# A hybrid decoder layer: TensorE in the order of the source, or in the scheduler's

## The chip, the cores and the metric

The kernel runs on one core of a Trainium2 chip. The metric is the device time of one execution in microseconds; three runs of the kernel before the change took 2751.72, 2754.8 and 2756.76 us, a median of 2754.8. One further execution was recorded by the hardware profiler, and all views below are of that one. The engines are called PE (TensorE, matrix products), PEld (its weight loads), DVE (VectorE), ACT (ScalarE), POOL (GpSimd) and SP (SyncE, which here issues the DMA transfers).

## The reference

One decoder layer over 2048 tokens of 1024 features, batch 1, all in float32:

```python
mod = silu(c) @ w_ada + b_ada                       # six vectors of 1024
sh1, sc1, ga1, sh2, sc2, ga2 = split(mod, 6)
h  = rms_norm(x, g_attn) * (1 + sc1) + sh1
z  = h @ w_in                                       # q, k, v of both head groups, gates
ya = swa_attention(...)          # 8 heads of 64, window 128, ALiBi, sinks, 2 kv heads
yb = forgetting_attention(...)   # 8 heads of 64, causal over all keys, F = cumsum(log_sigmoid(f))
x  = x + ga1 * (concat(ya, yb) @ w_out)
h2 = rms_norm(x, g_mlp) * (1 + sc2) + sh2
u  = causal_dwconv(h2 @ w_up, conv_w, conv_b)       # width 3, 5632 channels
a, g = split(u, 2)
x  = x + ga2 * ((silu(g) * a) @ w_down)
y  = rms_norm(x, g_final)
```

## The kernel before

The tokens are cut into four blocks of 512 (n = 0 to 3). Each block has three stages. s1 makes the projections (products at L623 and L651; L276 for the first block), s2 is the attention, s3 is the output projection, the MLP's up-projection with its convolution (products at L1301) and the down-projection (output and down-projection share L1183). Float32 operands are split into a high and a low part in a faster format (wh and wl, hh and hl, ph and pl, ah and al), and each dense product is three matrix products: high by high, high by low, low by high.

The attention of a block is a list of units. A unit of the forgetting attention (a head, or half the queries of a head for n = 2 and 3) makes its scores (s, L968), which ACT and DVE read, biased, into tiles t; DVE keeps their running maximum mx (L951, L959). PE transposes mx (mt, L993), DVE reduces it to m, and PE spreads m over all rows (mb, L1000). ACT copies that (mm, L1007), DVE subtracts it from each t (L1014), ACT takes the exponential (L1019), DVE adds up the sums acc (L1029). Then, group by group of 512 columns, ACT casts t into ph (L728), DVE makes pl (L729), and PE multiplies both by the values into one accumulator o (L1063, L1066). The sums are transposed (lt, L1039), inverted (rl) and spread (mb again); yo (L1072 to L1074) reads o and the unit is stored. There are 48 such units, 8 each for n = 0 and 1 and 16 each for n = 2 and 3. Units of the sliding-window attention (L798 to L868) follow them.

The order of the work is written out by hand. `merge(main, side, ratio)` pulls dense work from one generator, with its cost in microseconds at each `yield`, and slips attention steps from another between, so that the attention keeps to a set share of the dense work. `s2` decides the steps by a clock of its own (`clock`) and by tables of gaps and delays for each block (GAPS, TAS, TBS, LATS, SGAPS). So s2(0) stands among s1(1) and s1(2), s2(1) among s3(0), s2(2) among s1(3) and s3(1), s2(3) among s3(2); s3(3) has nothing beside it. The calls stand in the last lines of the function. "The last merge" below is s3(2) with s2(3).

The framework schedules at build time: on each engine it takes, of the instructions whose operands and buffers its own timing model has ready, the one that comes first in the source. The line `tc.manual_schedule(engines={PE})` holds PE to the order of the source instead. Here it covers the whole kernel. ACT, SP and POOL have no such line over the whole kernel, nor has DVE; two short stretches hold DVE (and in the first one SP) too: `first_groups` and the end of the last block.

PSUM, into which PE writes, is cut into four buffers "d" for dense sums, three "s" shared by scores, mt, mb, lt and the small sums sd, and one "o". The tiles ph and pl have three buffers each (PB), t has ten (NT).

Of the kernel before, what the change touches and what calls it, by code (L numbers as in the profile page):

```python
# [70 lines left out]
def tile_decoder_layer(  # L71
# [42 lines left out]
        return t[:, :w]  # L114

    nc.scalar.preload_act_table_set("exp_and_others")
    ctx.enter_context(tc.manual_schedule(engines={mybir.EngineType.PE}))

    def side_ps(w=512):
        t = pa.tile([P, 512], F32, tag="s", name="sd", bufs=3)  # L120
# [1439 lines left out]
```

## Time and profile before

| what | value |
|---|---|
| median of three runs | 2754.8 us |
| the profiled execution's own time | 2755.67 us |
| its span, first to last instruction | 2754.0 us |
| mean granted clock of TensorE | 0.967 |
| busy: PE, DVE, ACT | 2566.3, 1930.8, 1491.7 us |
| moved by DMA | 588.26 MB |

In the views a line number is that of the kernel before. A row of the timeline has start, length, engine, line, operation, output and inputs, sizes, count, and in brackets the idle time just before with what ended it. A row of waits reads: who waited for whom, total us, times, longest. In a group of instructions the numbers after the count are total busy us and mean ns of one, then the idle time just before them. PE's instructions overlap at their ends, so the price of one in a stream is the distance between two starts, not its length.

### The profile page before, as it was taken

The numbers are of one execution on the slowest core, as the hardware profiler recorded it, in microseconds if no ns is written. First come the engines' busy times: TensorE is split into PE (matmuls) and PEld (weight loads), VectorE is DVE, ScalarE is ACT, GpSimd is POOL, SyncE is SP. The second block draws the span as 40 slices with busy tenths as digits, with TensorE's granted clock in tenths as the row PEclk, the third lists the DMA queues.
The fourth block names the chain that finished last, engine by engine and source line by source line (L and its number), as shares of the span: only waits on it lengthen the run. The fifth ranks groups of instructions, "written<-read, shape, count | busy, mean of one in ns | idle before, by whom it ended". The sixth has DMA issues, their size and how long they took to land.

```text
span 2754.0 us, 38503 instructions
## 1 busy us (share of the span) xinstructions
PE 2566.3 (93%) x12852; PEld 2168.5 (79%) x12852; DVE 1930.8 (70%) x3813; ACT 1491.7 (54%) x3085; POOL 93.1 (3%) x171
## 2 busy tenths in 40 slices
PE   7999888799989999988999999989999999999998
PEld 5878786677877877877788887878888887788887
DVE  6467656789878657776888865879989876344433
ACT  5456564565556666556555665576666666422222
POOL 0001000100000000000000000100000000000000
PEclk9999999899999999999999999999999999999999
DMA  7967579756646786675667779735555576655564
GB/s 234 296 181 234 153 216 306 237 178 200 198 150 201 218 263 204 210 245 166 211 225 228 236 255 300 274 119 179 182 186 180 180 243 218 249 196 196 188 228 183
DMA packets 424515, 588.26 MB, mean 214 GB/s; under 512 B 32380, under 2 KB 272756, under 8 KB 424316
## 3 DMA queue, kind: packets, MB, share of 16 engines
q1 hardware_dynamic: 424316, 585.79, 65.8%
q8 instruction: 102, 1.67, 0.3%
q14 instruction: 97, 0.79, 0.1%
HBM read 440.95 MB, written 144.71 MB: 213 GB/s over the span
## 4 chain that ended last, share of the span: by engine, by line
PE 75%; DVE 8%; DMA 7%; ACT 5%; issue 2%; SPq 1%; POOL 1%; DVEq 0%; POOLq 0%; ACTq 0%
PE d L1301 33%; PE d L1183 19%; PE d L623 6%; PE s L968 4%; DMA wada<-in_w_ada_dram 2%; PE o L1063 2%; PE o L1066 2%; PE d L651 2%; DVE wl L379 1%; DMA q<-qd 1%; DMA wr<-in_w_in_dram 1%; PE mb L1000 1%; PE d L276 1%; PE s L798 1%; DVE pl L729 1%
## 5 line engine op out<-in xcount | busy, mean ns | idle before, releaser
L1301 PE MATMUL d<-hh,wkh 128*128 128x512 f32 (+1 forms) x920 | 355.4, 386 | 6.3 <-ACT hh L110 6.3
L1301 PE MATMUL d<-hl,wkh 128*128 128x512 f32 (+1 forms) x920 | 354.7, 386 | 3.7 <-DVE hl L538 2.7
L1301 PE MATMUL d<-hh,wkl 128*128 128x512 f32 (+1 forms) x920 | 352.1, 383 | 0.0
L379 DVE TENSOR_TENSOR wl<-wr,wh 128x1024 fp32r<-128x1024 f32 (+5 forms) x184 | 219.2, 1192 | 113.9 <-ACT wh L378 99.4
L728 ACT CAST ph<-t 128x512 fp32r<-128x512 f32 (+2 forms) x304 | 178.2, 587 | 188.8 <-PE o L1063 185.9
L378 ACT CAST wh<-wr 128x1024 fp32r<-128x1024 f32 (+5 forms) x184 | 188.5, 1025 | 169.0 <-PE d L1301 78.6
L985 ACT ACTIVATE t<-s,bc 128x256 f32<-128x256 f32 (+3 forms) x464 | 204.5, 480 | 103.3 <-DVE t L979 49.7
L1331 ACT ACTIVATE u<-d,cb,cw 128x512 f32<-128x512 f32 x176 | 136.7, 777 | 223.2 <-PE d L1301 217.7
L1334 DVE SCALAR_TENSOR_TENSOR u<-d,cw,u 128x511 f32<-128x511 f32 x176 | 130.8, 743 | 158.9 <-ACT u L1331 158.2
L729 DVE TENSOR_TENSOR pl<-t,ph 128x512 fp32r<-128x512 f32 (+2 forms) x304 | 195.8, 646 | 37.7 <-ACT ph L728 36.5
L1301 PE MATMUL d<-hh,wh 128*128 128x512 f32 (+1 forms) x552 | 215.7, 391 | 2.2 <-ACT hh L110 2.2
L1301 PE MATMUL d<-hl,wh 128*128 128x512 f32 (+1 forms) x552 | 214.2, 388 | 0.4
L968 PE MATMUL s<-q,kkb 128*128 128x256 f32 (+2 forms) x1024 | 198.6, 309 | 16.8 <-DMA q<-qd 16.8
L1301 PE MATMUL d<-hh,wl 128*128 128x512 f32 (+1 forms) x552 | 213.1, 386 | 0.0
L1301 PEld LDWEIGHTS d<-hh,wkh 128*128 128x128 f32 x920 | 174.4, 190 | 39.3 <-ACT hh L110 8.8
L1301 PEld LDWEIGHTS d<-hl,wkh 128*128 128x128 f32 x920 | 174.1, 189 | 38.1 <-DVE hl L538 7.5
L1301 PEld LDWEIGHTS d<-hh,wkl 128*128 128x128 f32 x920 | 174.2, 189 | 33.5
L1063 PE MATMUL o<-ph,vvb 128*128 128x256 f32 (+2 forms) x512 | 153.9, 318 | 27.7 <-DVE yo L1073 27.7
L1019 ACT ACTIVATE t<-t 128x512 f32<-128x512 f32 (+2 forms) x304 | 168.5, 598 | 13.4 <-DVE t L1018 7.2
L968 PEld LDWEIGHTS s<-q,kkb 128*128 128x128 f32 x1024 | 153.7, 197 | 24.5 <-DMA q<-qd 16.4
L623 PE MATMUL d<-hh,wh 128*128 128x512 f32 x360 | 146.2, 406 | 2.6 <-DVE lf L666 2.2
L623 PE MATMUL d<-hl,wh 128*128 128x512 f32 x360 | 143.9, 400 | 2.9 <-DVE hl L538 2.9
(232 smaller groups left out, 6128.5 us busy)
## 6 DMA issues: line engine op xcount, KB each, us to landing
wkh<-wsu SPq DMA_DIRECT2D x110, 512.0 KB
wkl<-wsu SPq DMA_DIRECT2D x110, 512.0 KB
wr<-in_w_up_dram SPq DMA_DIRECT2D x66, 512.0 KB
wkh<-wsd SPq DMA_DIRECT2D x55, 512.0 KB
wkl<-wsd SPq DMA_DIRECT2D x55, 512.0 KB
wr<-in_w_in_dram SPq DMA_DIRECT2D x49, 512.0 KB
wada<-in_w_ada_dram SPq DMA_DIRECT2D x96, 256.0 KB
wsu<-wh SPq DMA_DIRECT2D x44, 512.0 KB
```

What stands on the lines that cost most here:

```text
L378: nc.scalar.copy(wh, raw)
L379: nc.vector.tensor_sub(wl, raw, r32(wh))
L623: nc.tensor.matmul(ps, a[:, k, :], b[k], start=(k == 0 and i == 0), stop=(k == KT - 1 and i == 2),)
L728: nc.scalar.copy(ph[:, e0:], src[:, e0:])
L729: nc.vector.tensor_sub(pl[:, e0:], src[:, e0:], r32(ph[:, e0:]))
L968: nc.tensor.matmul(ps[:, o + low(c0) : o + w], st["kks"][kb // 4][:, (kb % 4) * P : (kb % 4 + 1) * P], qs[a][:, low(c0) : w], start=(a == ...
L985: nc.scalar.activation(tt[:, plain : o + w], ps[:, plain : o + w], AF.Identity, bias=bias(kb))
L1019: nc.scalar.activation(t1, t1, AF.Exp)
L1063: nc.tensor.matmul(po[:, c:], v, ph[:, o + c : o + w], start=(kb == 0), stop=False)
L1183: nc.tensor.matmul(acc[t], l[:, ts], r[:, k % 2, :], start=(i == 0 and l is ah and r is wh), stop=(i == n_k - 1 and l is al),)
L1301: nc.tensor.matmul(ps[:, c], w[a][:, k, :], b[k][:, c], start=(k == 0 and i == 0), stop=(k == KT - 1 and i == 2),)
L1331: nc.scalar.activation(u, ps, AF.Identity, bias=cb[:, ci : ci + 1], scale=c2)
```

## The change

One line goes: PE is no longer held to the source's order, and the framework's scheduler orders it as it does the other engines. Work, tiles, buffers and the source's order, which still gives the priorities, are the same. The two short stretches that hold DVE and SP stay.

```diff
     nc.scalar.preload_act_table_set("exp_and_others")
-    ctx.enter_context(tc.manual_schedule(engines={mybir.EngineType.PE}))
 
     def side_ps(w=512):
```

Of the 12,808 matrix products of the program 7,939 stand at another place in PE's order, 2,980 by more than 20 places and 449 by more than 100; the farthest comes 168 later and 233 earlier. The last 226 stand where they stood. DVE, ACT, POOL and SP have the same instructions in a changed order. In the changed kernel the line numbers are one lower behind the line that went, and the buffer numbers two lower: mb_21286 at L1000 becomes mb_21284 at L999.

The first place is in the last merge, on PE, ahead of a unit's mt. Before (16 rows of this list lie between the last score, s_20512, and mt):

```order
L1301 MATMUL d_20490<-hl_18457,wkh_20239 128x512
L1301 MATMUL d_20490<-hh_18456,wkl_20241 128x512
L1301 MATMUL d_20490<-hh_18468,wkh_20239 128x512
L1301 MATMUL d_20490<-hl_18469,wkh_20239 128x512
L1301 MATMUL d_20490<-hh_18468,wkl_20241 128x512
L1063 MATMUL o_20436<-ph_20462,vvb_19245 128x256
L1066 MATMUL o_20436<-pl_20463,vvb_19245 128x256
L1063 MATMUL o_20436<-ph_20462,vvb_19245 128x256
L1066 MATMUL o_20436<-pl_20463,vvb_19245 128x256
L993 MATMUL mt_20543<-ident_87,mx_20311 128x128 x2
L968 MATMUL s_20549<-q_20300,kkb_19928 128x256 x4
```

Now (60 rows lie between the last score, s_20510, and mt):

```order
L1300 MATMUL d_21030<-hl_18443,wkh_20776 128x512
L1300 MATMUL d_21030<-hh_18442,wkl_20778 128x512
L1300 MATMUL d_21030<-hh_18454,wkh_20776 128x512
L1300 MATMUL d_21030<-hl_18455,wkh_20776 128x512
L1300 MATMUL d_21030<-hh_18454,wkl_20778 128x512
L1300 MATMUL d_21030<-hh_18466,wkh_20776 128x512
L1300 MATMUL d_21030<-hl_18467,wkh_20776 128x512
L1300 MATMUL d_21030<-hh_18466,wkl_20778 128x512
L1065 MATMUL o_20434<-pl_20584,vvb_19253 128x256
L1062 MATMUL o_20434<-ph_20583,vvb_19253 128x256
L1065 MATMUL o_20434<-pl_20584,vvb_19253 128x256
L992 MATMUL mt_20541<-ident_85,mx_20309 128x128 x2
```

More dense products have come between the last score and mt, and the products o of the unit before are scattered among them.

The second place is two units later, on PE: the mb that spreads m, and the unit's first product o. Before, with the dense rows that follow; the unit's first product, o_21491, stands 64 rows of this list behind the last row here:

```order
L1063 MATMUL o_21128<-ph_21195,vvb_19942 128x256
L1066 MATMUL o_21128<-pl_21196,vvb_19942 128x256
L1063 MATMUL o_21128<-ph_21195,vvb_19942 128x256
L1066 MATMUL o_21128<-pl_21196,vvb_19942 128x256
L1000 MATMUL mb_21286<-ident_87,m_21238 128x128 x2
L968 MATMUL s_21336<-q_20992,kkb_20620 128x256 x4
L1301 MATMUL d_21264<-hh_18432,wkh_21028 128x512
L1301 MATMUL d_21264<-hl_18433,wkh_21028 128x512
```

Now the first product, o_21489, stands close behind mb:

```order
L1300 MATMUL d_21801<-hh_18466,wkh_21539 128x512
L1300 MATMUL d_21801<-hl_18467,wkh_21539 128x512
L1300 MATMUL d_21801<-hh_18466,wkl_21541 128x512
L999 MATMUL mb_21284<-ident_85,m_21236 128x128 x2
L967 MATMUL s_21334<-q_20990,kkb_20618 128x256 x4
L1038 MATMUL lt_21359<-ident_85,acc_20969 128x128 x2
L967 MATMUL s_21370<-q_20990,kkb_20626 128x256 x4
L967 MATMUL s_21411<-q_20990,kkb_20626 128x256 x4
L1062 MATMUL o_21489<-ph_21402,vvb_20619 128x256
L1300 MATMUL d_21872<-hh_18309,wkh_21621 128x512
L1300 MATMUL d_21872<-hl_18310,wkh_21621 128x512
L1300 MATMUL d_21872<-hh_18309,wkl_21623 128x512
```

Of the 48 long and the short products that stood between mb and the unit's first product, three scores of four products each and one pair of transposes lt are left.

The third place is in s3(0), on PE, where the sums sd over the last four chunks of the modulation vector stand between the output projection and the up-projection (without buffer numbers). Before:

```order
L1183 MATMUL d<-wh,yl 128x512
L209 MATMUL sd<-ones,acc 128x1 x16
L1063 MATMUL o<-ph,vvb 128x512
L1066 MATMUL o<-pl,vvb 128x512
L968 MATMUL s<-q,kkb 128x512 x2
L1039 MATMUL lt<-ident,acc 128x128 x4
L1063 MATMUL o<-ph,vvb 128x384
L1066 MATMUL o<-pl,vvb 128x384
L993 MATMUL mt<-ident,mx 128x128 x4
L968 MATMUL s<-q,kkb 128x512 x2
L1063 MATMUL o<-ph,vvb 128x256
L1066 MATMUL o<-pl,vvb 128x256
```

Now:

```order
L208 MATMUL sd<-ones,acc 128x1 x8
L967 MATMUL s<-q,kkb 128x512 x2
L1038 MATMUL lt<-ident,acc 128x128 x2
L992 MATMUL mt<-ident,mx 128x128 x2
L1038 MATMUL lt<-ident,acc 128x128 x2
L992 MATMUL mt<-ident,mx 128x128 x2
L967 MATMUL s<-q,kkb 128x512 x2
L208 MATMUL sd<-ones,acc 128x1 x4
L999 MATMUL mb<-ident,rl 128x128 x4
L999 MATMUL mb<-ident,m 128x128 x4
L208 MATMUL sd<-ones,acc 128x1 x4
L967 MATMUL s<-q,kkb 128x512 x6
```

The products o that stood behind sd now stand ahead of it, and scores, lt, mt and mb of the attention stand between its parts.

## The prediction, made blind

> **What bounds the kernel now.** I read the page's first part, then the stages, then who TensorE (PE) waits for.
>
> ```profile
> span 2754.0 us, 38503 instructions
> PE 2566.3 (93%) x12852; PEld 2168.5 (79%) x12852; DVE 1930.8 (70%) x3813; ACT 1491.7 (54%) x3085; POOL 93.1 (3%) x171
> PE 75%; DVE 8%; DMA 7%; ACT 5%; issue 2%; SPq 1%; POOL 1%; DVEq 0%; POOLq 0%; ACTq 0%
> ```
>
> PE is the bound: busy 93% and 75% of the chain that ended last. What an order of PE's instructions can win is at most its idle time, 2754.0 - 2566.3 = 188 us, and what the clock loses behind the longest waits. The stages show where that lies (columns: window, length, then busy time of PE, PEld, DVE, ACT, POOL with counts, granted clock, DMA share, GB/s):
>
> ```profile
> 500.00:700.00 200.00, 171.79 (x813) 142.71 (x812) 164.32 (x297) 109.55 (x207) 9.61 (x12) 0.91 0.62 191
> 1900.00:2100.00 200.00, 195.45 (x1065) 168.03 (x1064) 183.16 (x370) 123.76 (x265) 1.44 (x7) 1.00 0.54 181
> 2100.00:2300.00 200.00, 192.72 (x1030) 164.24 (x1029) 164.95 (x355) 132.46 (x307) 0.82 (x4) 0.99 0.65 211
> 2394.00:2754.00 360.00, 351.32 (x1562) 291.08 (x1561) 144.65 (x244) 81.34 (x127) 4.98 (x8) 0.99 0.56 199
> ```
>
> Early on there is much to win: 28 us idle in 500 to 700, at clock 0.91. In 1900 to 2100 there is next to nothing: PE idles 4.5 us, and VectorE (DVE) is at 183.16 of 200, so it cannot catch up either if it falls behind. The last 360 us are one dense stream; there the change's order differs only in small places. The waits by name:
>
> ```profile
> PE o L1063 <- DVE yo L1073: 27.7, 9, 7.5
> PE mt L993 <- DVE mx L959: 20.9, 12, 4.5
> PE s L968 <- DMA q<-qd: 16.8, 4, 10.1
> PE sd L209 <- DVE acc L201: 14.3, 2, 8.7
> PE o L851 <- DVE yo L868: 11.6, 7, 4.0
> PE mt L993 <- DVE mx L951: 5.8, 2, 5.0
> ```
>
> (Total us, times, longest.) These six make 97 of the idle time. In each, dense products that were ready stand in the source behind an attention instruction that was not.
>
> **What it wins.** One mechanism: where the planned attention instruction was not ready, the scheduler has put dense products ahead of it.
>
> The waits of mt (transposes of a unit's running maximum, 26.7 us together). A pair of units of the last merge is typical:
>
> ```profile
> 2061.59 0.44 PE L993 MATMUL mt<-ident,mx 128*128 128x128 f32 x2 [1.52 <-DVE mx L959]
> 2061.79 0.73 PE L968 MATMUL s<-q,kkb 128*128 128x256 f32 x4
> 2068.54 0.39 PE L1301 MATMUL d<-hl,wkh 128*128 128x512 f32 x1
> 2068.77 0.39 PE L1301 MATMUL d<-hh,wkl 128*128 128x512 f32 x1
> ```
>
> A long product costs 2068.77 - 2068.54 = 0.23 us of PE in a stream. In the source 12 of them and four short ones lie between a unit's last score and its mt, about 3.3 us; in the changed order about 12 us at the place shown above in the part on the change, and a median near 8 over all 48 units. Where a unit waited and its new distance is larger, I count the smaller of the wait and the added distance: 23 of the 26.7 us (0 to 27).
>
> The waits of the one PSUM buffer "o" (27.7 + 11.6 = 39.3 us): the next unit's first product waits until yo has read the last unit's sums. The median of PE work between the two grows from 4.4 to 7.2 us, but the worst one, after the last dense row of a stage, stays. I take 24 (0 to 39).
>
> The queries:
>
> ```profile
> 473.47 7.42 DMA q<-qd
> ```
>
> A score waited 10.1 us for this load. Its second half now stands 11 us of PE work later. With two smaller ones I take 13 (0 to 17).
>
> The sums of the modulation vector:
>
> ```profile
> 521.82 1.86 PE L209 MATMUL sd<-ones,acc 128*128 128x1 f32 x8 [5.57 <-DVE acc L201]
> 532.40 1.86 PE L209 MATMUL sd<-ones,acc 128*128 128x1 f32 x8 [8.71 <-DVE acc L201]
> 534.12 0.77 PE L1063 MATMUL o<-ph,vvb 128*128 128x512 f32 x1
> ```
>
> All later dense work needs these sums, so only attention can stand in between. The changed order puts two scores, lt, mt and mb there and some products ahead: 5 us (0 to 8); the weights' arrival still sets the rest.
>
> Small waits of dense products:
>
> ```profile
> PE d L1301 <- ACT hh L110: 8.5, 13, 3.5
> PE d L623 <- DVE hl L538: 2.9, 5, 2.0
> PE d L1183 <- DVE al L1288: 2.9, 2, 2.2
> PE d L1301 <- DVE hl L538: 2.7, 5, 0.8
> ```
>
> Of these 17 us I count 12, again the smaller of wait and added distance (0 to 17). Sum won: 23 + 24 + 13 + 5 + 12 = 77. The clock: 500 to 700 lost 0.09 x 200 = 18 us of clock around 28 us of idle time, part of it while PE stood still anyway, so I take half a us per us of a long stall. About 30 of the 77 are long ones: 15 more, 92 in all.
>
> [...]
>
> **What it costs.** The scheduler places an instruction as soon as it believes the operands ready, with no margin. PE works its rows in order, so a row placed too early stops the dense rows behind it too. In the source the attention has a margin, which this chain shows (from mb, which spreads a unit's maximum, to the first product of that unit):
>
> ```profile
> 2065.57 0.38 PE L1000 MATMUL mb<-ident,m 128*128 128x128 f32 x2
> 2066.18 0.37 ACT L1007 COPY mm<-mb 128x256 f32<-128x256 f32 x1
> 2066.91 4.30 DVE L1014 TENSOR_TENSOR t<-t,mm 128x512 f32<-128x512 f32 x7
> 2067.63 1.84 ACT L1019 ACTIVATE t<-t 128x512 f32<-128x512 f32 x3 [0.27 <-DVE t L1014]
> 2070.56 0.61 ACT L728 CAST ph<-t 128x512 fp32r<-128x512 f32 x1
> 2073.33 0.68 DVE L729 TENSOR_TENSOR pl<-t,ph 128x512 fp32r<-128x512 f32 x1
> 2080.55 0.28 PE L1063 MATMUL o<-ph,vvb 128*128 128x256 f32 x1
> 2080.67 0.28 PE L1066 MATMUL o<-pl,vvb 128*128 128x256 f32 x1
> ```
>
> The operands are there at 2073.33 + 0.68 = 2074.0, some 8 us after mb has ended, and PE comes for them at 2080.55: 6.5 us of margin. (A short product costs PE 2080.67 - 2080.55 = 0.12 us in a stream.) That ACT waits for PE here, and not PE for ACT, shows over the program:
>
> ```profile
> L728 ACT CAST ph<-t 128x512 fp32r<-128x512 f32 (+2 forms) x304 | 178.2, 587 | 188.8 <-PE o L1063 185.9
> L729 DVE TENSOR_TENSOR pl<-t,ph 128x512 fp32r<-128x512 f32 (+2 forms) x304 | 195.8, 646 | 37.7 <-ACT ph L728 36.5
> ```
>
> A, first products. In the changed order of this same unit 12 short scores and two transposes lie between mb and the first product, 12 x 0.12 + 4 x 0.10 = 1.8 us with mb's own (0.10 is half of the way from mt's start to the next row's, 2061.59 to 2061.79). Five units of the last merge have 1.7 to 4.5 us there (1.8, 3.5, 1.7, 4.5, 1.7). Against 8 us this leaves 6 + 5 + 6 + 4 + 6 = 27 us of PE standing still. From below, the chain with no queue is 0.37 + 0.61 + 0.61 + 0.61 + 0.68 = 2.9 us, and three units would lose about 4 together. I take 27, as DVE runs seven subtractions in one block before it comes to pl.
>
> B, the other products of the units. Before, 12 long products (2.8 us) lay between two groups of products. Now there are stretches of ten and more dense ones, and then several groups at once. A group needs four DVE operations (subtract, add, pl, maximum) of 4.30 / 7 = 0.61 us in a stream, 2.5 us. A unit has 7 or 8 groups, 18 us of DVE. Two units took 2123.4 - 2061.6 = 61.8 us, 30.9 each:
>
> ```profile
> 2123.41 0.44 PE L993 MATMUL mt<-ident,mx 128*128 128x128 f32 x2 [1.52 <-DVE mx L959]
> ```
>
> The changed order leaves the last units of this merge 24 to 26 us of PE work each, with the MLP's own operations on DVE besides. If I move each product by as much as its distance from mb changes, and set that against its margin in the trace, the margins of the 48 units are overdrawn by 90 us with A's 27, in 700 to 900 and 1750 to 2250. So 0 (the margin measured so is often just the wait for a free buffer) to 63. I take 45, nearer the top, for DVE's 183.16 of 200 leaves it no room to make up.
>
> C, smaller ones: score tiles begun and ended 11 us later hold one of three PSUM buffers, and hh and al are wanted earlier in places. By the same count 0 to 30; I take 20.
>
> The clock, half a us for each us in stalls over 3 us, some 28 of these: 14.
>
> Sum lost: 27 + 45 + 20 + 14 = 106. **Net: 106 - 92 = 14 us slower.** Against the profiled execution's 2755.7 us that is 2769.7; this execution lies 0.9 above the median of the runs, so 2769.
>
> At nothing I cost the loads: SP's rows move by at most 24 places, no wait of PE above names a weight, and the DMA engines stand at 0.54 in 1900 to 2100. The dense rows come up to 117 places, 27 us, earlier; were that cover gone, one weight load would be late by a landing as above, 7 us.
>
> **Rivals.**
>
> Faster. The scheduler's idea of the operations' times is good enough, and its early rows find their operands. For it: in 29 of the 48 units the margins stay positive, and the first 900 us hold most of the long waits. Against it: 1750 to 2250, above. With A at 4, B and C at 15 together and 20 us of gain given back where waits only change their place: -92 + 19 + 20 = -53, about 2703.
>
> No change: wins and losses cancel. The two sums differ by less than the bounds of B alone. 2755.
>
> Much slower. In the last merge DVE sets the pace: dense rows put ahead bring the convolution's DVE work ahead of the maxima and subtractions, and all sixteen units, not five, lose A's 6.4 us. It decides from the point where DVE, at 183 of 200 now, is full. 11 x 6.4 = 70 more: about 2840.
>
> PE passes waiting rows by itself, so the order matters little: the row at 534.12 speaks against this; it carries no wait of its own, yet started only when the sums ahead of it were through. [...] That the change does nothing is out: 7,939 of 12,808 products stand at another place.
>
> **How the numbers follow.** My forecast, 2769, has 0.38; much slower 0.13; no change (passing included) 0.13; faster 0.36. What a measurement here can tell from no change is about 0.2%, 5.5 us. So slower by more 0.51, within 0.13, faster 0.36. The forecast's own range is 2761 (B at 36) to 2797 (B and C at their tops). To hold eight in ten the range reaches to 2690 below (the faster case with half of the 20 given back kept) and 2860 above (much slower with C at its top).
>
> **What will show it.** Right: mt's and yo's waits fall to a third; the wait of the score for q is gone; first products (L1062 after the change) become a new named wait for ph and pl of 25 us and more, in 1750 to 2250; that stretch gets longer, and 500 to 900 shorter. The last 360 us stay within 3. It is wrong if 1750 to 2250 gets no longer, which would make A and B a mistake, or if mt and yo wait as before, which would take the wins away.

## The result, and the profile after

The changed kernel takes 2674.45 us (median of 4 runs, 2667.54 to 2677.57); the kernel before, run on the same chip, 2755.78 (2751.72 to 2761.66). The ratio is 0.971, with a 95% interval from 0.968 to 0.973: 3% faster. The prediction was 14 us slower, with 2690 as the low end of its range: wrong in sign and outside the range.

The page of the changed kernel begins (its own time is 2671.37 us):

```profile
span 2669.7 us, 38426 instructions
PE 2547.5 (95%) x12852; PEld 2157.9 (81%) x12852; DVE 1919.8 (72%) x3813; ACT 1471.9 (55%) x3085; POOL 91.3 (3%) x171
PE 78%; DMA 8%; DVE 6%; ACT 4%; issue 1%; SPq 1%; POOL 1%; POOLq 0%; DVEq 0%; ACTq 0%
```

PE still bounds it. Its idle time fell from 188 to 2669.7 - 2547.5 = 122 us, and for the same products it was busy 19 us less. Whom PE waits for, in the lines that answer to those of before (total us, times, longest):

```profile
PE o L1062 <- DVE yo L1072: 0.9, 2, 0.8
PE o L850 <- DVE yo L867: 0.7, 1, 0.7
PE mt L992 <- DVE mx L950: 1.6, 2, 0.9
PE s L797 <- DMA q<-qd: 1.5, 1, 1.5
PE d L524 <- ACT x1row L110: 14.7, 4, 7.8
PE d L1300 <- DVE halo L1344: 8.7, 3, 3.3
PE o L1065 <- DVE pl L728: 8.2, 11, 1.3
PE d L1182 <- ACT ah L1286: 6.4, 6, 2.4
```

The waits on yo (39.3 us before), on mx (26.7) and on q (16.8) are as good as gone, and the waits of the sums sd on acc (14.3) are no longer named. The lower four lines are new or have grown; together they stay far below what went.

Where the time went is seen when both traces are cut at the same two products: the end of block 2's output projection, where the dense half of the last merge goes over to the MLP, and the end of block 2's down-projection. The windows of the kernel before (columns as in the prediction):

```profile
0.00:1780.50 1780.50, 1635.19 (x8192) 1381.54 (x8193) 1296.81 (x2573) 1027.62 (x2104) 68.26 (x125) 0.96 0.71 224
1780.50:2327.70 547.20, 518.75 (x2806) 444.84 (x2805) 461.38 (x949) 353.38 (x787) 10.59 (x22) 0.98 0.56 185
2327.70:2754.00 426.30, 412.33 (x1858) 342.13 (x1856) 172.65 (x292) 110.73 (x194) 14.25 (x24) 0.98 0.58 208
```

And of the changed kernel:

```profile
0.00:1676.40 1676.40, 1606.02 (x8182) 1362.59 (x8183) 1280.74 (x2560) 1007.29 (x2089) 66.46 (x125) 0.98 0.75 238
1676.40:2245.50 569.10, 530.67 (x2813) 453.00 (x2812) 466.14 (x960) 354.83 (x802) 10.45 (x22) 0.95 0.54 178
2245.50:2669.70 424.20, 410.84 (x1860) 342.33 (x1859) 172.90 (x295) 109.75 (x194) 14.42 (x24) 0.98 0.58 209
```

In the first stretch the change is 104.1 us ahead: PE idles 74.9 us less (145.3 to 70.4), and is busy 29.2 us less with the same products to within ten. Most of that is the clock (0.96 to 0.98): of PE's busy time 100.5 us fell into spells of half clock before and 54.8 now. In such a spell a long product costs 0.43 us in a stream (2003.59 to 2004.02 in the changed kernel) where 0.23 is usual, so about half of the difference, 22.9 us, is the clock's by estimate. The second stretch is the last merge without its output projection, which lies ahead of the cut. There it gives back 21.9 us: 10.0 more of idle time and 11.9 more of busy time, at a clock of 0.95 where it was 0.98. The rest is within 2.1 us. So the change has two parts of opposite sign, with a border between them in the program.

### The profile page after: what moved, and what is told of

It is laid out like the page before. It is cut to its first block, busy times and chain, and to the rows that moved or that the text cites. A ratio compares the mean times of both kernels' runs of the same rounds, so it can differ in the third digit from the quotient of the medians.

```text
span 2669.7 us, 38426 instructions
## 1 busy us (share of the span) xinstructions
PE 2547.5 (95%) x12852; PEld 2157.9 (81%) x12852; DVE 1919.8 (72%) x3813; ACT 1471.9 (55%) x3085; POOL 91.3 (3%) x171
## 4 chain that ended last, share of the span: by engine, by line
PE 78%; DMA 8%; DVE 6%; ACT 4%; issue 1%; SPq 1%; POOL 1%; POOLq 0%; DVEq 0%; ACTq 0%
PE d L1300 36%; PE d L1182 19%; PE d L622 7%; PE s L967 4%; PE d L650 2%; PE o L1065 2%; PE o L1062 2%; DMA wada<-in_w_ada_dram 2%; DMA zrow<-zd 1%; DVE t L1013 1%; PE mb L999 1%; DMA yraw<-yd 1%; PE d L275 1%; DMA wr<-in_w_in_dram 1%; PE s L797 1%
## 5 line engine op out<-in xcount | busy, mean ns | idle before, releaser
L1062 PE MATMUL o<-ph,vvb 128*128 128x256 f32 (+2 forms) x512 | 150.7, 310 | 10.3 <-ACT t L1018 3.4
L1065 PE MATMUL o<-pl,vvb 128*128 128x256 f32 (+2 forms) x512 | 146.2, 305 | 8.2 <-DVE pl L728 8.2
```

The costliest lines, as they stand in the source:

```text
L1062: nc.tensor.matmul(po[:, c:], v, ph[:, o + c : o + w], start=(kb == 0), stop=False)
L1065: nc.tensor.matmul(po[:, c:], v, pl[:, o + c : o + w], start=False, stop=(kb == nkb - 1))
```

## The experiments

Times are medians; each run's kernel before, on the same chip, lay between 2751.7 and 2754.2 us.

### The last merge alone

```diff
+    with tc.manual_schedule(engines={mybir.EngineType.PE}):
-    merge(s3(2, [lambda: yprep(3, 1)]), s2(3), RM[3] * att_cost(3) / 383.0)
+        merge(s3(2, [lambda: yprep(3, 1)]), s2(3), RM[3] * att_cost(3) / 383.0)
```

(in the changed kernel), and the converse: the same line left free, each of the other merges put under such a `with`.

> The changed kernel with PE held to the source order in one place, the last merge (the up-projection and first half of the down-projection of block 2 beside the attention of block 3). Theory 1, the change wins in the first three merges and loses in the last: of the 104 us that it was ahead at 1676 us it gave back 22 before the last block began, so about 2674 - 22 = 2652 (2644 to 2660); in the last merge the waits of d for a halo read (8.7 us, three of about 3) go, and mt waits for mx again, some 9 us. Rival: what is lost there is owed to work that the first three merges only put off (attention and VectorE behind), and comes whatever the order of the last merge: 2668 to 2680.

> The converse: PE held to the source order in all merges but the last. Theory 1: only the loss is left, 2756 + 22 = 2778 (2768 to 2790). Rival (the loss belongs to what the first three merges put off): the last merge gains like the others, by the mt waits of that merge, some 9 us: 2740 to 2752.

Held in the last merge: 2657.56 us, ratio 0.966 [0.964, 0.967], 17 us below the changed kernel by the medians and 14 by the ratios, and the fastest version here that computes the reference. Free only there: 2768.61, ratio 1.006 [1.004, 1.008], 16 us slower than before. The loss belongs to the free order of the last merge, wherever the rest stands; by the times its size is 14 to 17 where 22 was expected. The held version's windows:

```profile
0.00:1681.90 1681.90, 1611.03 (x8192) 1366.36 (x8193) 1287.91 (x2573) 1014.45 (x2104) 65.64 (x125) 0.98 0.75 237
1681.90:2231.50 549.60, 520.37 (x2806) 446.00 (x2805) 461.48 (x949) 353.25 (x787) 10.57 (x22) 0.98 0.57 184
2231.50:2654.40 422.90, 409.83 (x1859) 341.43 (x1857) 171.54 (x292) 109.27 (x194) 14.36 (x24) 0.99 0.58 209
```

The first stretch keeps 98.6 of the 104.1 us, and the second is back within 2.4 us of the kernel before: 19.5 us shorter than in the changed kernel. The waits of d for halo are gone there, and those of mt for mx are back with 9.7 us. Where only this merge is free, its stretch is

```profile
1764.30:2338.40 574.10, 534.27 (x2812) 456.30 (x2811) 467.16 (x963) 355.33 (x801) 11.36 (x22) 0.95 0.54 176
```

or 26.9 us longer than before, more than the 16 of the times. The difference lies ahead of the cut: that trace was 16.2 us ahead at 1764.3, although up to 1710 PE's order differs from that of before only in some hundred places between 125 and 146 us. By the same estimate from busy time at half clock 12.5 of the 16.2 are the clock. Why is not shown, so the clock's part of a difference between two traces is uncertain by about as much here.

### Two of the winning merges alone

The same `with` around all merges but one: that of blocks 1 and 2's input stage, or that of block 0's MLP.

> PE left to the scheduler in one merge only, that of blocks 1 and 2's input stage with block 0's attention; held to the source in all others. Theory 5, each merge's gain is its own: the changed kernel was 37.3 us ahead when the output projection of block 0 ended, and this run keeps that: 2753 - 37 = 2716 (2708 to 2724), with the waits of s for q gone. Rival: a merge's gain needs free order in the merges beside it, since work is put off over their borders; then under half is kept: 2735 or more.

> The same for the next merge alone, block 0's MLP stages with block 1's attention. Theory 5: the changed kernel gained 22.3 us in the up-projection of block 0 and 9.8 in its down-projection, so 2753 - 32 = 2721 (2713 to 2729); the waits of sd for acc fall from 14 us to under 5. Rival: under half: 2737 or more.

2720.70 us, ratio 0.988 [0.986, 0.991], and 2717.14, ratio 0.986 [0.984, 0.989]: 31 and 35 us gained where 37 and 32 were expected. Each merge has its own gain; together 66, where the changed kernel was 69.5 us ahead at the end of block 0's MLP. The traces agree: cut at the start of block 0's output projection (450 us before) and at the end of its MLP (1039.3), the freed stretches are 29.1 and 42.7 us shorter than before, those of the changed kernel 24.9 and 44.6. The next merge, block 3's input stage and block 1's MLP beside block 2's attention, gave 34.6 us of the 104.1 in the changed kernel and has no run of its own. One detail was wrong: the 10 us wait for q did not go with the first of the two, as PE's waits in that kernel show,

```profile
PE s L967 <- DMA q<-qd: 12.5, 3, 10.3
PE sd L208 <- DVE acc L200: 11.4, 2, 6.7
```

but with the second, whose line is

```profile
PE s L967 <- DMA q<-qd: 4.1, 2, 2.9
```

and there the wait of sd on acc is no longer named. The wait for q stands inside block 0's output projection, and that belongs to the second of the two merges.

### Two of the waits taken away in the source's own order

In the kernel before: `QB = 3` becomes `QB = 4`; and in another run `TAS = [1.5, 3, 4, 2]` becomes `TAS = [1.5, 5, 6, 5]`.

> The kernel before with four buffers for q instead of three, all else held to the source. The prediction's term of 13 us for the queries: the score's wait of 10.1 us and most of the three others go, with the half-clock spell of 10 us behind it: 2752 - 10 to 17, about 2739 (2735 to 2744). Rival: the load is late for another reason (its data or its queue) or PE then waits at the same place for the sums of the modulation vector, which all later dense work needs: 2748 to 2756.

> The kernel before, PE held to the source throughout; only the planner's distance from a unit's last score to mt grows for blocks 1 to 3 (3, 4, 2 become 5, 6, 5), which lengthens the PE work in between from 4.7 to about 10 us, 4.9 to 9.9 and 3.3 to 7.1. Theory 2, the gain is that of the waits named, which any order with more distance has too: mt's waits fall from 26.7 us to under 8, and the time by as much and half of the clock behind the 5 us ones, to about 2733 (2725 to 2742). Rival: the waiting only changes its place (to o or to the first products), 2750 to 2762.

Four buffers: 2740.30 us, ratio 0.995 [0.993, 0.997], 13.9 us gained; no wait on q is left among the named ones, and the trace went from 0.8 us behind to 11.1 ahead as that place was passed. But the sums that follow waited longer, one of them 15.9 us where 8.7 was the longest:

```profile
PE sd L209 <- DVE acc L201: 17.1, 2, 15.9
```

Behind them the trace was 5.3 us ahead, and the rest of the 13.9 came later. So the rival's second half, that PE would then wait for the sums, holds for about half of the gain at that place; that all of it would go there is refuted by the time.

mt later: 2742.44, ratio 0.996 [0.994, 0.999], 9.8 us gained, short of the 23 expected. The waits did go; PE's lines for mt are now

```profile
PE mt L993 <- DVE mx L951: 4.9, 2, 4.4
PE mt L993 <- DVE mx L959: 4.5, 3, 2.9
```

or 9.4 us where 26.7 stood, and at the end of the first half of block 2's down-projection its trace was 43.5 us ahead of the kernel before. Then it lost 30.6 us before block 3's output projection was through. Some 17 us of that is more busy time, for 731 products stand in that stretch where 634 stood before: part of the lead was attention work left for later. The other 13 are idle time (17.0 us against 3.6), with these waits of PE in and just ahead of it (the same view, for 2113.3 to 2358.8 alone):

```profile
PE o L851 <- DVE yo L868: 9.4, 3, 6.4
PE lt L1039 <- DVE acc L1032: 3.5, 1, 3.5
```

Later maxima make the last merge's attention end later, and there the dense work to cover it has run out. The order shows it: the last product of block 3's forgetting attention has 84 more products ahead of it than in the kernel before, some 20 us of PE work by estimate, at up to 0.23 us each; in the changed kernel it has two fewer. So theory 2 holds in the middle of the merges and the rival at the end of the last one.

### What an early product waits for

In the kernel before, block 3 only: `len(held) > DEPTH` becomes `len(held) > (0 if n == 3 else DEPTH)`, and the last of `LATS = [0, 2, 2, 2]` becomes -3. The products of a unit then stand 3.3 us of work behind mb in half of the units, instead of 13.6.

> The kernel before, PE held to the source throughout; only in the attention of block 3 the source puts a unit's first product earlier: the PE work between mb and it falls from 11 to 15 us (half are 13.6) to 3.3 for half of the units, 0.1 and 1.9 for two, 7.4 for six. The rule of the prediction's term A, PE stands still for 8 us less this work: 8 units x 4.7 + 6.1 + 7.9 + 6 x 0.6 = 55 us in new waits of o for ph and pl, and half of it in the clock: 2756 + 55 + 25 = 2836 (2805 to 2845). Rival: the 8 us are what ACT and VectorE take when PE does not come, because their copies wait for a free buffer; a product that comes early gets its ph after mm, one subtraction, one exp and one copy, 3.2 us in the trace of before: waits under 12 us, 2750 to 2768.

2892.35 us, ratio 1.051 [1.049, 1.053]: 140 us slower, far above both. The named waits:

```profile
PE mb L1000 <- DVE rl L1048: 47.4, 17, 6.8
PE o L1066 <- DVE pl L729: 40.0, 10, 4.4
PE o L851 <- ACT ph L728: 21.9, 16, 5.1
PE o L1063 <- ACT ph L728: 8.9, 5, 4.2
```

The rule of term A is right for pl: 40 us in ten waits of up to 4.4, where 4.7 each was worked out, and with ph's 8.9 the units' own waits are 49, near the 55. The rival, that the 8 us are only ACT and VectorE waiting for a free buffer, is refuted. The other 69 us I had not seen: a unit whose products come early also wants its row sums (rl) early, and the sliding-window units (L851) their ph. But in the same units ph (8.9) was far less late than pl (40). Hence the next run, with each group's pl products one group behind its ph products:

```diff
+                    if g > 0:
+                        rows(g - 1, sm["pl"], True)
+                    rows(g, ph, False)
+                    sm["pl"] = pl
+                    if g == len(steps) - 1:
+                        rows(g, pl, True)
```

(`rows` issues a group's products with ph or with pl; this replaces the loop over both, for block 3.)

> The kernel with block 3's products early in the source order (2892 us), with one thing more: each group's pl products stand in the source one group later than its ph products, so that the PE work between mb and the first pl is 6.7 us (half of the units), 11.1 (six), 5.4 and 12.1, where it was 3.4, 7.5, 2.1 and 0.2; the first ph stays at 3.3. Theory 4, the 8 us of term A are pl's, and ph is there some 3 to 4.5 us after mb: o's waits for pl fall from 40 us to under 12, those for ph stay under 10 in block 3's forgetting attention, and the time falls by 28 us and some 10 of clock, to about 2855 (2840 to 2870). Rival: ph is as late as pl when PE comes early, and the waiting moves to the ph products: 2880 to 2900.

PE's waits in it (L1064 issues both kinds of product):

```profile
PE mt L993 <- DVE mx L959: 33.5, 16, 5.9
PE o L1064 <- ACT ph L728: 8.7, 5, 3.4
PE o L1064 <- DVE pl L729: 7.5, 7, 1.6
```

pl's waits fall to 7.5 us and ph's stay at 8.7, as expected: in these units it is pl that takes the 8 us after mb, and ph comes well before it. The time, 2872.57 us (ratio 1.043 [1.040, 1.045]), fell by 20, not 37, and lies just above the range of theory 4: 16 of the 32 us went over to mt, which waited 17.2 us in the run before this one.

### VectorE's part in the last merge

Both kernels have this in place of `elif g > 1:` (and a maximum with 1e-6 on rl); one is held in the last merge, one free. It leaves out 72 of the additions to block 3's row sums, so the output of that block is not the reference's.

```diff
+                elif g > 1 and (n < 3 or g == len(steps) - 1):
```

> The changed kernel with the last merge held to the source order, and less work for VectorE in it: in block 3's forgetting attention the running sum takes only a unit's first two groups and the last one (72 additions of about 0.61 us, 44 us of VectorE, are left out, and 16 small maxima guard the reciprocals; the row sums and so the output are wrong for block 3). It is the partner of the next run. By the theory that the held order waits for nothing of these additions it stays within 6 us of 2657.6; if VectorE limits the held order too, it gains 10 or more.

> The same additions left out, with the last merge left to the scheduler as in the changed kernel. Theory 3, the last merge loses because VectorE is full there, so that dense rows put ahead find their PSUM buffers not yet read: with 44 us of VectorE less, the waits of d for halo fall from 8.7 us to under 3 and the difference to the held partner from +17 us to between -6 and +5. Rival, the order itself loses (attention is pushed behind dense rows and must be made up without cover): the difference stays between +11 and +18.

Held 2645.02 us (2636.35 to 2646.82), free 2650.61 (2642.06 to 2658.14). The waits of d for halo are no longer named in the free one, and the difference falls from 14 to 17 us to 5.6, just outside the range of theory 3 and below the rival's. But the runs of each spread over 10 and 16 us, and four of each do not tell 5.6 from nothing, or from 14. The traces, cut at the same two products as above, say more, the held one first:

```profile
1674.30:2212.00 537.70, 518.71 (x2806) 443.51 (x2804) 424.75 (x896) 354.77 (x787) 8.91 (x22) 0.98 0.57 188
1680.30:2225.60 545.30, 519.49 (x2804) 444.71 (x2803) 428.23 (x908) 352.38 (x798) 10.91 (x22) 0.97 0.56 185
```

The free order's stretch is 7.6 us longer than the held one's, where it was 19.5 with all additions. So VectorE's load is the larger part of the loss, as far as one pair of traces can show it; since the scheduler also chose another order for the lighter program, the rest is left open. The held one gained 12.5, so VectorE limits it a little too.

## Why the prediction was wrong

**The wins were right in kind and too small in size.** mt, yo and q fell as the text said they would, to 1.6 of 26.7, 1.6 of 39.3 and 1.5 of 16.8 us; the run with four buffers gained 13.9 in all, its clock included, against q's term of 13. yo was mis-sized most: 24 was taken, 38 went, in part because the longest wait (7.5), behind the last dense row of a stage, which I had left standing, went too. The sums were put at 5 of 14.3; all of it went, and 3.0 came back as a wait of s for mod. Two lines that the sum did not have went as well; here as they stand in the kernel before:

```profile
PE d L651 <- DVE vst L663: 9.4, 8, 2.4
PE d L1183 <- DVE halo L1345: 6.9, 2, 5.7
```

They are now 2.1 and nothing. And the clock gave some 23 us in the first stretch where 15 was counted for the whole program.

**Terms A and B failed, 72 us of the loss.** In the changed kernel the products o wait 8.2 us for pl (above) and, in PE's lines for L1062 beside yo's,

```profile
PE o L1062 <- ACT t L1018: 3.4, 1, 3.4
PE o L1062 <- DVE es L818: 2.6, 1, 2.6
PE o L1062 <- DMA wkl<-wsu: 2.2, 1, 2.2
PE o L1062 <- ACT ph L727: 1.2, 2, 0.9
```

some 18 us in all, and the first of these lines stands in a unit that had stood still for 3.6 us at that point before the change. Term A's step "the operands are there at 2074.0, some 8 us after mb has ended" took pl's time for the first product. The first product needs only ph, and that unit's own row has ph ready at 2070.56 + 0.61 = 2071.2. The very order shown above for that unit says so: behind o_21489<-ph_21402 stands a dense row, not o<-pl, and 21 dense products follow before pl is wanted. The timeline of the changed kernel at that place (start, length, engine, line; in brackets the idle time before and what ended it):

```profile
1994.21 0.38 PE L999 MATMUL mb<-ident,m 128*128 128x128 f32 x2
1995.83 4.29 DVE L1013 TENSOR_TENSOR t<-t,mm 128x512 f32<-128x512 f32 x7
1995.99 0.74 PE L967 MATMUL s<-q,kkb 128*128 128x256 f32 x4 [0.20 <-ACT t L984]
1998.26 0.62 ACT L727 CAST ph<-t 128x512 fp32r<-128x512 f32 x1
1998.93 0.38 PE L1062 MATMUL o<-ph,vvb 128*128 128x256 f32 x1 [2.21 <-DMA wkl<-wsu]
2000.38 0.73 DVE L1336 SCALAR_TENSOR_TENSOR u<-d,cw,u 128x510 f32<-128x510 f32 x1
2002.31 0.20 DVE L1344 SCALAR_TENSOR_TENSOR halo<-d,cw,halo 128x1 f32<-128x1 f32 x1
2002.57 0.80 PE L1300 MATMUL d<-hh,wkh 128*128 128x512 f32 x1 [3.25 <-DVE halo L1344]
2003.04 1.28 DVE L728 TENSOR_TENSOR pl<-t,ph 128x512 fp32r<-128x512 f32 x2
```

The product waits 2.2 us, not 6, and starts as ph ends (1998.26 + 0.62; the weight load that the profile names came last by its record, though the product does not read it). Over the five units of term A the standing still ahead of the first product, counted by the prices of a stream, comes to 3.5, 0.4, 2.4, 0 and 1.1 us: 7.4 where 27 was taken, and nearer to the 4 that the prediction had as its bound from below. Term B is mis-sized in the same way: of its 45 us some 11 came, pl's 8.2 and, for a first product outside the five units (at 819.6 us), the 2.6 that the profile puts down to es. Its margins were overdrawn on paper in 700 to 900 too; PE idles 3.8 us there in the changed kernel's windows (the second row is for below):

```profile
700.00:900.00 200.00, 196.16 (x940) 162.41 (x939) 170.01 (x346) 135.78 (x287) 0.62 (x3) 0.98 0.67 206
...
2045.10:2149.40 104.30, 97.62 (x522) 83.43 (x520) 88.24 (x167) 62.63 (x136) 0.82 (x4) 0.93 0.51 164
```

A margin seen in a held order is no price. There ACT waited 185.9 us over the program with its next ph for PE to free a buffer; in the changed kernel's costliest groups that line is

```profile
L727 ACT CAST ph<-t 128x512 fp32r<-128x512 f32 (+2 forms) x304 | 176.7, 590 | 115.1 <-PE o L1062 113.6
```

so ACT is still mostly the one that waits.

**What the last merge really loses** stands in the same trace. Its idle time grew by 10.0 us. Seven subtractions of the unit hold VectorE from 1995.83 to 2000.12; the convolution's reads of a finished up-projection row (L1336, L1344) queue behind them until 2002.51; and the next row, now put close behind, finds no free d buffer until then: 3.25 us, three times in this merge. That is the mechanism of the rival "much slower", with the row of d and not the first product as its victim, and 8.7 us and not 70. Other new waits of this merge, on pl (5.0), ph (with the lines beside it 6.8), ah (4.0) and x1row (7.8 where 4.2 stood), are about made up by those that went, mt's 13.4 and yo's 6.8 first. The second part of the loss is the clock, close to the forecast's 14 us: 11.9 more of busy time. By the busy time at half clock (16.4 us before, 38.2 now) 10.9 of it are the clock, again by estimate, half of that in the up-projection (granted clock 0.98 before, 0.95 now) and a third in the first half of block 2's down-projection (0.98 before, 0.93 in the second row of windows above). The forecast's 14 us count half a us for each us in stalls over 3 us, and no run shows that limit: here 10.9 us of clock came with 10.0 us more of idle time, and the clock fell at 2051.9 behind waits of 0.85 and 1.19 us (last section).

**The other signs.** 500 to 900 is shorter; the stretch behind 1750 did get longer, by 21.9 us; the last merge is the only place that loses; the last 360 us differ by less than 3. The sign "o at L1062 waits 25 us and more" failed, and with it the net. With A at 7 and B at 11 in place of 27 and 45, the prediction's own sum is 52 - 92 = -40, which has the sign; yo (14), the two lines that it left out (14) and the clock of the first stretch (8) are 36 of the 41 that are left to -81. The match is rough: waits that grew elsewhere, x1row's from 5.2 to 14.7 first, are not in it, and term C's 20 us were not measured by themselves.

## What to carry to other kernels

An order fixed by hand for the engine that bounds is worth testing per stage: here the free order won 31 and 35 us in two merges and lost 14 to 17 in the last one, where a second engine had little room (VectorE, busy 183 of 200 us in 1900 to 2100 before the change), and holding just that merge beat both. When the cost of an earlier instruction is read from a trace, take the moment at which its own operand is ready, not that of its pair, and look in the new order at what stands between the two. A margin that ends in a wait for a buffer is not a need; it bounds the loss from above only.

## What was not expected of the hardware

Here the clock fell without a long wait. In the changed kernel's first half of block 2's down-projection four idle times of 0.85, 1.19, 1.12 and 1.5 us lie within 9 us (2048 to 2056.7). The clock falls at 2051.9: the first two, which end at 2048.8 and 2050.8, lie ahead of that, the other two behind it. The longest idle time ahead of the fall, from the end of the last spell at 2041.6 on, was 1.19 us. PE's waits for 2045.1 to 2062:

```profile
PE o L1065 <- DVE pl L728: 3.2, 3, 1.2
PE d L1182 <- ACT ah L1286: 1.5, 1, 1.5
```

The granted clock is at half from 2051.9 to 2062.1. Its window, with the spell at the wait of 3.25 us for comparison:

```profile
2000.70:2007.50 6.80, 4.93 (x12) 3.87 (x13) 6.80 (x15) 4.25 (x9) 0.00 (x0) 0.50 0.00 0
2051.90:2062.10 10.20, 7.58 (x25) 6.04 (x24) 9.69 (x21) 5.05 (x12) 0.00 (x0) 0.50 0.29 82
```

In the records of the clock 18 of the 19 such spells of the changed kernel last 3.41 us or a whole multiple of it, up to 11 times; the last, at 2662.9, goes on beyond the span. Half of their length within the span comes to 73 us, against 90 before the change (28 spells) and 56 with the last merge held (16).
